# A weight block's wide and narrow products by turns, in a two-layer hybrid diffusion backbone

## The chip, the cores and the metric

The kernel runs on one core of one Trainium2 chip. The metric is the device time of one execution in microseconds. Before the change the median of three runs is 2560.39 us (2558.62 to 2562.19).

## The reference

Two layers over 512 latent tokens and 256 context tokens of width 1024, in float32. Each layer normalises the tokens with a modulation that comes from a conditioning vector, projects them once, and feeds three mixers side by side: windowed attention, a gated linear attention in chunks, and a two-dimensional neighbourhood attention. Their outputs are projected, gated by a sigmoid of the normalised input, summed and projected again; a SwiGLU feed-forward of hidden width 2816 follows. Cut to its frame:

```python
for layer in range(2):
    h = rmsnorm(x) * (1 + scale) + shift            # latents and context, own modulation
    p = h @ w_in[layer]                             # split among the three mixers
    y_a, y_b, y_c = window(p), linear(p), neighbourhood(p)
    gates = sigmoid(h @ w_merge + b_merge)          # three of width 1024
    x = x + gate * ((g_a * (y_a @ w_ba) + g_b * (y_b @ w_bb) + g_c * (y_c @ w_bc)) @ w_out)
    h = rmsnorm(x) * (1 + scale) + shift
    x = x + gate * ((silu(h @ w_gate) * (h @ w_up)) @ w_down)
```

In the second layer the context serves keys, values and the linear attention's state only; its later parts run over the 512 latents alone.

## The kernel before

Tokens lie along the free axis, features along the partitions. All big projections go through `gemm` (L370): one weight block holds 128 output features, with eight k tiles of 128 input features as a rule (four in the branch projections, `w_br`; six in the last part of the feed-forward's output). Float32 accuracy comes from splitting both operands into a high and a low half of type float32r: each k tile takes three products, `wh` with the high half of the tokens, `wh` with the low half, and `wl` with the high half. A moving operand is one of the token sets of the list `subs`: the 512 latents, called wide here, and where the context is needed the 256 context columns, called narrow. A set's products for one block form a chain that adds up in one PSUM bank; a copy out of the bank on ACT or DVE (`evac`) follows it.

A block runs the chain of the latents and then the chain of the context: 24 products and 24 products. PSUM buffers come from `gemm_psum` (L492). In the mixers there are three, named `g`; in the merge and the feed-forward (`wide`) four more, named `h`. The same `g` buffers hold the modulation vector of a later layer part while it adds up over eight small blocks (`ada`, `adp_tile`, L466 and L487), which `weave` spreads between the weight blocks of the mixers.

Weights come by DMA into `wr` (three buffers, queue SP), are cast to `wh` by ACT (L323), and `wl` is the rest, formed by DVE (L326). In the middle of each chain `ahead` starts the cast of a later block, and at the chain's end `split_lo` issues its low half and frees the raw block for the next DMA. At most two split blocks wait.

The emitter keeps a clock of TensorE's work. Generators (the linear attention, the norms, the stream of attention heads) are stepped by `tick` between products when their time has come, at the earliest each 0.5 us of that clock, and put their own products, copies and DVE work into the same engines' queues. All engines take their queues in order. A scheduler behind the emitter keeps its order as a rule; where products would wait for operands, as at the start of the merge, it lets the products of several blocks pass each other.

Copies out of the banks that the text speaks of: L554 and L559 (merge-gate logits, latents and context, one ACT copy each), L724 (projection blocks, one ACT copy), L1093 to L1110 (query and key stacks of the attention, four to ten ACT and DVE instructions).

Of the kernel before, what the change touches and what calls it, by code (L numbers as in the profile page):

```python
# [28 lines left out]
LEADQ = (1, 0)  # L29
LAG, GRAIN, QLAG = (0.7, 0.0, 0.5), 0.5, (0.0, 4.7)  # L30
# [5 lines left out]
# block numbers of the input projection after layout_inputs  # L36
AQ, AK, AV, GQ, GK, GV, GR, NQ, NK, NV = 0, 4, 5, 6, 8, 10, 14, 18, 22, 26
# sections of the modulation vector
# [3 lines left out]
def shape_constants():  # L42
    """Masks and rotary tables: functions of the shapes alone."""
    f = np.float32
# [40 lines left out]
def layout_inputs(i):  # L85
    """Reorders, slices and zero-pads the inputs; no value is changed."""
# [15 lines left out]
    # units of 1024 columns: two of halves of (shift, scale) of the mixer, then a section each  # L102
# [32 lines left out]
class Net:  # L135
# [23 lines left out]
    def psum_open(self, name, **bufs):  # L159
        """PSUM of a phase: s2 pairs of banks, p single ones."""  # L160
        self.pp = self.phx.enter_context(self.tc.tile_pool(name=name, bufs=bufs["s2"], space=PSUM))
# [4 lines left out]
    def hilo(self, hi, lo, src):  # L166
        """hi + lo == src, each with float32r's bits; src float32."""
        self.nc.scalar.copy(hi, src)  # L168
        self.nc.vector.tensor_tensor(out=lo, in0=src, in1=hi.bitcast(F32), op=ALU.subtract)

    def hilo_late(self, hi, lo, src):
        """hilo whose lo comes in the middle of the next product, when hi is there."""
        self.nc.scalar.copy(hi, src)  # L173
        self.late.append((lo, lambda: self.nc.vector.tensor_tensor(out=lo, in0=src, in1=hi.bitcast(F32),
                                                                   op=ALU.subtract)))
# [6 lines left out]
    def rsqrt(self, y, v, t):  # L182
        """y = v ** -0.5 (v > 0) by Newton steps from an exponent-halving start."""
# [13 lines left out]
    # The emitter keeps a clock of the tensor engine's work. Generators are fillers: each yields the time (us of  # L197
    # that clock) its next step's inputs need; the products between step them when it has passed.
# [18 lines left out]
    def tick(self):  # L217
        """Steps the fillers that are due; False if none was."""
# [24 lines left out]
    def room(self, what, limit):  # L243
        """Steps the fillers until fewer than limit of what are in use."""
        self.until(lambda: self.live.get(what, 0) < limit)

    def attend(self, units, delay=0.0):
        """Queues units of a head for the attention stream."""
# [8 lines left out]
    def stream(self):  # L257
        """Scores of a unit, values product of the head before, transposes of the unit before, by turns."""
# [31 lines left out]
    def run_items(self):  # L290
        """Runs the items in order; weight blocks are loaded and split ahead of the product that takes them."""
# [17 lines left out]
        def split_hi(k):  # L309
            """Splits the next block, if it is due by block k and has room; its lo part with split_lo."""  # L310
# [59 lines left out]
    def gemm(self, w, nk, subs):  # L370
        """subs: (moving(kt) -> (hi, lo), columns, evacuate(psum))."""
        def sub(wh, wl, mov, n, evac):
            ps = self.gemm_psum()
            for kt in range(nk):
                xh, xl = mov(kt)
                if any(lo.tensor is xl.tensor for lo, _ in self.late):
# [3 lines left out]
                self.matmul(ps[:, :n], wh[:, s], xh, start=kt == 0, stop=False)  # L380
                self.matmul(ps[:, :n], wh[:, s], xl, start=False, stop=False)
                self.matmul(ps[:, :n], wl[:, s], xh, start=False, stop=last)
# [3 lines left out]
                if self.clock > self.ticked + self.grain and not last:  # L386
                    self.tick()
            self.split_lo()
# [3 lines left out]
        def fn(wh, wl):  # L392
            for x in subs:
                sub(wh, wl, *x)
# [51 lines left out]
    def consts_rest(self):  # L446
# [12 lines left out]
        # relative biases shifted by the query's column i: [i, (layer, head, row offset), key column]  # L459
# [6 lines left out]
    def ada(self, l, units):  # L466
        """Units of the modulation vector of layer l: 1024 channels by eight items of a k tile; columns 256 g on
        go to rows 32 * g on."""
# [30 lines left out]
    def ada_cols(self, l, n, sb):  # L499
        nc = self.nc  # L500
        pm = self.O1()
        # [channel, (column group, half of it, stream)]
# [26 lines left out]
    def cap(self, f):  # L529
        """The items f adds, taken off the list."""  # L530
# [5 lines left out]
    def weave(self, main, side):  # L536
        """Adds main's items with side's spread between the GEMM blocks."""
# [11 lines left out]
    def zgates(self, l, blocks, ntok):  # L549
        """Logits of the merge gates, kept in DRAM until the merge."""  # L550
# [16 lines left out]
    # Two sets of tokens: (first column, end, stream)  # L567
    SETS = (((0, SEQ, 0), (SEQ, NT, 1)), ((0, 256, 0), (256, SEQ, 0)))

    def sq_add(self, x, kt, c):  # L570
        """Adds the squares of x's columns c (feature tile kt) to the running sums of their set."""
# [12 lines left out]
    def rstd_rows(self, c):  # L584
        """Generator: rstd of the tokens c, the same on all partitions; self.rows: SBUF tile, columns c."""
# [25 lines left out]
    def norm(self, l, which, c, new, early=False):  # L611
        """Generator: modulated RMS norm of the tokens c of self.x into self.h, (hi, lo) tiles (new: allocates
        them)."""
# [9 lines left out]
        if early:  # L623
            # (x is read again later: scaled in place, while the modulation is still to come)
# [7 lines left out]
        for kt in range(KT):  # L632
# [7 lines left out]
            if kt % 2 == 0:  # L640
                # t + bi, as hi + lo
# [25 lines left out]
    def hmov(self, l, which, c):  # L667
        """Moving operand: the tokens c of the norm's output, once it is there."""
# [12 lines left out]
    def win(self, l, b, lat, ctx):  # L681
        """One block of the input projection; lat / ctx evacuate their columns (None: not needed)."""
# [33 lines left out]
    def in_block(self, l, b, dst, scale=1.0, ctx=True):  # L716
        """(weights, sub, subs): a block of the input projection, scaled, into the tile dst()."""
# [11 lines left out]
    def gla_lead(self, l):  # L729
        """The first blocks of the input projection, a token set after the other: the second set's norm runs  # L730
        beside the first's products."""
# [19 lines left out]
    def gemm_low(self, l, c, tile_):  # L751
        """The 32 columns of the decays' inner rank; k tile kt adds to rows 32 * (kt % 4) on (the sum over the
        four groups of rows is the next product's)."""
# [39 lines left out]
    def gate_r(self, l):  # L793
        """The output gate of the linear attention, kept in DRAM until the merge."""
# [25 lines left out]
    def gla_unit(self, l, u, slot, want_o):  # L820
        """u = 0, 1: the latents of head pair u, four chunks of 128; u = 2: the context of both pairs, two
        chunks each.  Blocks b of 128 tokens: b = chunk, or b = 2 * pair + chunk."""
# [3 lines left out]
        # slices of the [128, 512] unit: (columns of the unit, tile index, columns of the tile)  # L826
# [8 lines left out]
        # log decays (times 16)  # L835
# [23 lines left out]
        def qbd(n, f):  # L859
            """Writes f(out, rows, columns, tile, columns of the tile) for both heads of the pair."""  # L860
# [10 lines left out]
        def products(kap, qt, other=False):  # L871
            """Keys of each half of a chunk with the queries of that half (or of the other one):
            [token of the chunk, (block, head), query of the half]."""
# [32 lines left out]
        def prep(n, s):  # L906
            """Factors of level n (pairs of blocks of s), then the sums over blocks of 2 s."""
# [41 lines left out]
        # whole chunks: factors towards the state  # L949
# [26 lines left out]
        # states  # L976
# [17 lines left out]
        for d in range(2):  # L994
# [8 lines left out]
            else:  # L1003
                # context: states before the second chunk go to st[:, d, b]
# [740 lines left out]
```

## Time and profile before

| | |
|---|---|
| median of three runs | 2560.39 us |
| span of the profiled execution | 2559.8 us |
| TensorE busy (PE) | 2483.4 us, 97%, 14908 products |
| weight loads (PEld) | 2089.3 us, 82% |
| VectorE busy (DVE) | 1396.2 us, 55% |
| ScalarE busy (ACT) | 1041.1 us, 41% |
| GpSimd busy (POOL) | 353.7 us, 14% |

The span runs from the first to the last instruction of one profiled execution; its own time is not given apart from the span, and the timed runs lie within 3 us of it. A matmul's printed duration includes the way through the array and overlaps the next one, so the distance from one start to the next is what it costs. In a time line, neighbouring rows of one kind are merged, also products of both widths if their names agree (the form shown is then the first one's), and the count stands behind the `x`. A product of plain float32, as those of the modulation vector, counts twice in it.

### The profile page before, as it was taken

The page shows a single profiled execution, that of the slowest core. Times are in us where ns is not written, and L with a number is a line of the kernel's source. Part 1 is how long each engine was busy: PE and PEld are TensorE (multiplying, and loading weights), DVE is VectorE, ACT ScalarE, POOL GpSimd, SP SyncE. Part 2 cuts the span into 40 slices and gives each one's busy share as a digit, 9 for nine tenths or more (in the row PEclk, how much of TensorE's full clock was granted, in tenths as well). Part 3 has the DMA queues.
Part 4 walks back from the last instruction along what each step waited for, and adds up shares of the span by engine and source line. Part 5 has one row for each costly group of instructions (what it writes and reads, how often), then busy time and mean ns, then how long its engine had stood idle before and what let it go on. Part 6 is the DMA issues. An engine that isn't in the chain of part 4 may idle for free.

```text
span 2559.8 us, 38398 instructions
## 1 busy us (share of the span) xinstructions
PE 2483.4 (97%) x14908; PEld 2089.3 (82%) x14908; DVE 1396.2 (55%) x2832; ACT 1041.1 (41%) x1717; POOL 353.7 (14%) x447
## 2 busy tenths in 40 slices
PE   6999999999999999999999999999999999999998
PEld 3777878888888888888888877677888879988887
DVE  4683547647656674222232377746657668633336
ACT  3533336545565353212212255434545565522223
POOL 0230204213212010000000022212313220000000
PEclk9999999999999999999999999999999999999999
DMA  6333452232337332221221243453332275432333
GB/s 219 123 119 121 159 165 86 85 120 81 88 131 244 126 116 91 66 65 59 66 66 58 86 135 127 152 186 113 103 95 80 81 239 182 156 99 96 94 95 120
DMA packets 116422, 300.44 MB, mean 117 GB/s; under 512 B 21520, under 2 KB 31504, under 8 KB 116240
## 3 DMA queue, kind: packets, MB, share of 16 engines
q1 hardware_dynamic: 116240, 297.99, 36.5%
q8 instruction: 117, 1.92, 0.3%
q14 instruction: 65, 0.53, 0.1%
HBM read 258.61 MB, written 29.57 MB: 113 GB/s over the span
## 4 chain that ended last, share of the span: by engine, by line
PE 82%; DVE 10%; ACT 4%; issue 1%; DMA 1%; SPq 0%; POOL 0%; DVEq 0%; ACTq 0%; POOLq 0%
PE g L211 44%; PE h L211 26%; PE s L211 5%; PE s L215 3%; PE o L211 3%; DVE qbd L918 2%; DVE wl L326 1%; PE p L211 1%; DVE T L582 1%; DVE T L645 0%; ACT wh L323 0%; DVE SS L928 0%; DVE PP L930 0%; DVE PP L929 0%; DVE T L626 0%
## 5 line engine op out<-in xcount | busy, mean ns | idle before, releaser
L211 PE MATMUL g<-T,wh 128*128 128x512 f32 (+1 forms) x4684 | 1237.3, 352 | 6.6 <-ACT wh L323 3.4
L211 PEld LDWEIGHTS g<-T,wh 128*128 128x128 f32 x4684 | 801.5, 190 | 129.4 <-issue 20.4
L211 PE MATMUL g<-T,wl 128*128 128x512 f32 (+1 forms) x2342 | 816.1, 349 | 11.4 <-DVE wl L326 11.3
L211 PE MATMUL h<-T,wh 128*128 128x512 f32 (+1 forms) x2612 | 660.2, 343 | 4.9 <-ACT T L168 4.7
L323 ACT CAST wh<-wr 128x1024 fp32r<-128x1024 f32 (+2 forms) x355 | 344.4, 971 | 686.8 <-PE h L211 268.0
L326 DVE TENSOR_TENSOR wl<-wr,wh 128x1024 fp32r<-128x1024 f32 (+2 forms) x355 | 403.6, 1137 | 360.4 <-ACT wh L323 346.9
L211 PEld LDWEIGHTS h<-T,wh 128*128 128x128 f32 x2612 | 450.5, 189 | 70.9 <-ACT T L168 6.5
L211 PEld LDWEIGHTS g<-T,wl 128*128 128x128 f32 x2342 | 444.6, 190 | 72.3 <-DVE wl L326 15.1
L211 PE MATMUL h<-T,wl 128*128 128x512 f32 (+1 forms) x1306 | 447.6, 343 | 2.5 <-DVE wl L326 2.5
L211 PEld LDWEIGHTS h<-T,wl 128*128 128x128 f32 x1306 | 247.2, 189 | 32.9 <-DVE wl L326 2.9
L1270 ACT ACTIVATE P<-P,sm 128x513 f32<-128x513 f32 (+3 forms) x160 | 115.9, 725 | 127.8 <-DVE sm L1312 113.6
L1275 POOL TENSOR_SCALAR P<-P,sm 128x512 f32<-128x512 f32 (+1 forms) x160 | 113.4, 710 | 386.3 <-DVE sm L1274 363.8
L652 POOL TENSOR_TENSOR T<-T,T 128x256 f32<-128x256 f32 (+1 forms) x24 | 30.0, 1272 | 731.6 <-DVE T L1555 532.0
L1325 DVE TENSOR_TENSOR ptl<-s,pth 128x512 fp32r<-128x512 f32 (+1 forms) x144 | 107.9, 749 | 39.2 <-ACT pth L1324 38.0
L1324 ACT CAST pth<-s 128x512 fp32r<-128x512 f32 (+1 forms) x144 | 90.6, 629 | 46.8 <-PE s L215 43.4
L1555 DVE SCALAR_TENSOR_TENSOR T<-h,mod,T 128x512 f32<-128x512 f32 (+1 forms) x64 | 38.4, 599 | 110.1 <-PE h L211 110.0
L215 PE MATMUL s<-k_ident,P 128*128 128x128 f32 x640 | 94.0, 274 | 1.7 <-POOL P L1275 1.2
L921 POOL TENSOR_TENSOR E<-E,T 128x512 f32<-128x512 f32 (+1 forms) x42 | 59.5, 1426 | 247.1 <-ACT E L917 209.7
L173 ACT CAST T<-T 128x512 fp32r<-128x512 f32 (+1 forms) x93 | 49.1, 535 | 107.0 <-DVE T L1574 100.0
L215 PEld LDWEIGHTS s<-k_ident,P 128*128 128x128 f32 x640 | 74.6, 140 | 16.4 <-issue 4.8
L918 DVE TENSOR_TENSOR qbd<-E,T 64x512 f32<-64x512 f32 (+1 forms) x84 | 72.1, 871 | 3.6 <-ACT E L917 2.2
L211 PE MATMUL o<-pth,V 128*128 128x512 f32 (+2 forms) x224 | 72.5, 333 | 0.2 <-ACT pth L1324 0.2
(201 smaller groups left out, 2302.0 us busy)
## 6 DMA issues: line engine op xcount, KB each, us to landing
wr<-in_w_fi_dram SPq DMA_DIRECT2D x98, 512.0 KB, 3.6
wr<-in_w_ada_dram SPq DMA_DIRECT2D x80, 512.0 KB, 4.1
wr<-in_w_in_dram SPq DMA_DIRECT2D x65, 512.0 KB, 3.9
wr<-in_w_merge_dram SPq DMA_DIRECT2D x48, 512.0 KB, 4.2
wr<-in_w_out_dram SPq DMA_DIRECT2D x32, 512.0 KB, 3.6
wr<-in_w_fo_dram SPq DMA_DIRECT2D x32, 512.0 KB, 3.5
wr<-in_w_br_dram SPq DMA_DIRECT2D x48, 256.0 KB, 2.9
wr<-in_w_fo_dram SPq DMA_DIRECT2D x32, 384.0 KB, 3.1
```

The source lines that it names most:

```text
L173: self.nc.scalar.copy(hi, src)
L211: return self.nc.tensor.matmul(out, lhsT, rhs, **kw)
L215: return self.nc.tensor.transpose(out, src, self.ident)
L323: self.nc.scalar.copy(hi[:, :n], r[:, :n])
L326: self.nc.vector.tensor_tensor(out=lo[:, :n], in0=r[:, :n], in1=hi[:, :n].bitcast(F32), op=ALU.subtract)
L918: qt = qbd(n + 1, lambda o, r, c0, c1, q: V.tensor_tensor(out=o, in0=blk(ee[r, 0, c0:c1]), in1=blk(q), op=ALU.mult))
L921: P.tensor_tensor(out=ee[:, 1, c0:c1], in0=ee[:, 1, c0:c1], in1=self.gk[p][:, t0:t0 + c1 - c0], op=ALU.mult)
L1270: nc.scalar.activation(out=P_[:, o0:e1], in_=P_[:, o0:e1], func=AF.Exp, bias=nm_, accum_out=rz)
L1275: nc.gpsimd.tensor_scalar(out=P_[:, o0:o1], in0=P_[:, o0:o1], scalar1=rz, scalar2=1.0, op0=ALU.mult, op1=ALU.mult)
L1324: nc.scalar.copy(hi, src)
L1325: return lambda: VE.tensor_tensor(out=lo, in0=src, in1=hi.bitcast(F32), op=ALU.subtract)
L1555: self.nc.vector.scalar_tensor_tensor(out=x[:, c0:c1], in0=ps[:, :c1 - c0], scalar=self.mod[l][:, sec * 8 + j, s:s + 1], in1=x[:, c0:c1], ...
```

## The change

`gemm` now makes each set's chain a generator that stops after every product. A small loop starts the first chain, lets it run `BEHIND = 6` products, starts the second, and then takes one product of each by turns until both are done. A block with one set runs as before. The chains' other duties (`ahead` in the middle, `split_lo` and the copy out at the end, `tick`) stay with their chain. The PSUM buffer is now taken after the first `mov(kt)`.

```diff
+BEHIND = 6
...
     def gemm(self, w, nk, subs):
-        def sub(wh, wl, mov, n, evac):
-            ps = self.gemm_psum()
+        def chain(wh, wl, mov, n, evac):
+            ps = None
             for kt in range(nk):
                 xh, xl = mov(kt)
+                if ps is None:
+                    ps = self.gemm_psum()
...
                 self.matmul(ps[:, :n], wh[:, s], xh, start=kt == 0, stop=False)
+                yield
                 self.matmul(ps[:, :n], wh[:, s], xl, start=False, stop=False)
+                yield
                 self.matmul(ps[:, :n], wl[:, s], xh, start=False, stop=last)
                 if kt == nk // 2 - 1:
                     self.flush()
                     self.ahead(False)
                 if self.clock > self.ticked + self.grain and not last:
                     self.tick()
+                if not last:
+                    yield
             self.split_lo()
             evac(ps)
             self.tick()

         def fn(wh, wl):
-            for x in subs:
-                sub(wh, wl, *x)
+            todo = [chain(wh, wl, *x) for x in subs]
+            n, live = 0, []
+            while todo or live:
+                if todo and n >= (len(subs) - len(todo)) * BEHIND:
+                    live.append(todo.pop(0))
+                live = [g for g in live if next(g, 0) is None]
+                n += 1
         self.items.append(Item(fn, w, nk))
```

The rest of the diff takes comments and docstrings away; line numbers move by a few.

First place: TensorE, a block of merge-gate logits in the first layer's linear attention, where its second set begins. `g` is the result bank, `T` a token tile (high or low half), `wh` and `wl` the halves of the weight block. Before:

```order
L211 MATMUL g294_2308<-T70_386,wh285_2229 128x512
L211 MATMUL g294_2308<-T69_385,wl286_2230 128x512
L211 MATMUL g294_2308<-T71_390,wh285_2229 128x512
L211 MATMUL g294_2308<-T72_391,wh285_2229 128x512
L211 MATMUL g294_2308<-T71_390,wl286_2230 128x512
L211 MATMUL g299_2341<-T44_279,wh285_2229 128x256
L211 MATMUL g299_2341<-T45_280,wh285_2229 128x256
L211 MATMUL g299_2341<-T44_279,wl286_2230 128x256
```

After:

```order
L212 MATMUL g292_2288<-T46_283,wl287_2236 128x512
L212 MATMUL g292_2288<-T48_288,wh286_2235 128x512
L212 MATMUL g295_2316<-T44_279,wh286_2235 128x256
L212 MATMUL g292_2288<-T49_289,wh286_2235 128x512
L212 MATMUL g295_2316<-T45_280,wh286_2235 128x256
L212 MATMUL g292_2288<-T48_288,wl287_2236 128x512
L212 MATMUL g295_2316<-T44_279,wl287_2236 128x256
L212 MATMUL g292_2288<-T50_293,wh286_2235 128x512
L212 MATMUL g295_2316<-T46_283,wh286_2235 128x256
L212 MATMUL g292_2288<-T51_294,wh286_2235 128x512
L212 MATMUL g295_2316<-T47_284,wh286_2235 128x256
```

Before, the context's first product stands behind the latents' last one; after, it stands behind the latents' seventh, and from there on the two banks alternate (128x512 and 128x256).

Second place: TensorE, the end of the same block and the start of the next, whose first bank is `g307`. `g267` is the bank of the modulation vector, `p` a product of the linear attention. Before:

```order
L211 MATMUL g299_2341<-T70_386,wh285_2229 128x256
L211 MATMUL g299_2341<-T69_385,wl286_2230 128x256
L211 MATMUL g299_2341<-T71_390,wh285_2229 128x256
L211 MATMUL g299_2341<-T72_391,wh285_2229 128x256
L211 MATMUL g299_2341<-T71_390,wl286_2230 128x256
L211 MATMUL g267_2072<-wr287_2245,cpad_72 32x256 x4
L211 MATMUL g267_2072<-wr292_2300,cpad_72 32x256 x4
L211 MATMUL g307_2406<-T44_279,wh295_2321 128x512
```

After:

```order
L212 MATMUL g292_2288<-T71_390,wl287_2236 128x512
L212 MATMUL p300_2359<-qbd0_1_708,E285_2218 64x128 x8
L212 MATMUL g295_2316<-T67_380,wl287_2236 128x256
L212 MATMUL g295_2316<-T69_385,wh286_2235 128x256
L212 MATMUL g295_2316<-T70_386,wh286_2235 128x256
L212 MATMUL g295_2316<-T69_385,wl287_2236 128x256
L212 MATMUL g295_2316<-T71_390,wh286_2235 128x256
L212 MATMUL g295_2316<-T72_391,wh286_2235 128x256
L212 MATMUL g295_2316<-T71_390,wl287_2236 128x256
L212 MATMUL g267_2072<-wr288_2263,cpad_72 32x256 x4
L212 MATMUL g267_2072<-wr290_2280,cpad_72 32x256 x4
L212 MATMUL g307_2406<-T44_279,wh296_2327 128x512
```

Before, all 24 products of the context lie between the latents' last product and the next block; after, the latents' last product stands seven context products ahead of the block's end.

Third place: ACT, the copies out of the same two banks (`T298` and `T299` are the logits), among the weight cast and the exponentials of the linear attention. Before:

```order
L323 CAST wh295_2321<-wr293_2306 128x1024
L554 COPY T298_2339<-g294_2308 128x512
L916 ACTIVATE E301_2357<-PP261_2030 128x32x16
L917 ACTIVATE E301_2357<-SS262_2031 128x32x16
L559 COPY T298_2339<-g299_2341 128x256
```

After:

```order
L324 CAST wh296_2327<-wr291_2286 128x1024
L568 COPY T299_2357<-g292_2288 128x512
L930 ACTIVATE E301_2368<-PP262_2045 128x32x16
L931 ACTIVATE E301_2368<-SS263_2046 128x32x16
L573 COPY T299_2357<-g295_2316 128x256
```

The order on ACT is the same: the cast of a later block stands ahead of the copy of the latents, two exponentials ahead of the copy of the context.

## Rows read from the trace of the kernel before

**Rows 1.** The page, busy time of each engine, and granted clock in 40 slices:

```profile
PE 2483.4 (97%) x14908; PEld 2089.3 (82%) x14908; DVE 1396.2 (55%) x2832; ACT 1041.1 (41%) x1717; POOL 353.7 (14%) x447
...
PEclk9999999999999999999999999999999999999999
```

**Rows 2.** The page, chain that ended last, shares of the span by engine:

```profile
PE 82%; DVE 10%; ACT 4%; issue 1%; DMA 1%; SPq 0%; POOL 0%; DVEq 0%; ACTq 0%; POOLq 0%
```

**Rows 3.** Windows of the first layer: length, busy time of PE, PEld, DVE, ACT, POOL:

```profile
91.00:375.00 284.00, 272.39 (x1969) 218.35 (x1969) 164.58 (x285) 106.30 (x159) 52.04 (x49) 0.99 0.40 131
375.00:768.00 393.00, 387.42 (x2501) 340.38 (x2499) 249.72 (x745) 214.19 (x438) 100.09 (x169) 1.00 0.32 101
768.00:1504.00 736.00, 729.30 (x4185) 637.83 (x4186) 313.93 (x466) 221.45 (x325) 37.77 (x28) 1.00 0.31 97
```

**Rows 4.** Waits of PE over the span: us in total, times, longest:

```profile
PE g L211 <- DVE wl L326: 11.3, 8, 3.7
...
PE g L211 <- ACT T L554: 0.5, 1, 0.5
```

**Rows 5.** Time line of PE, feed-forward; start, length, instruction, count:

```profile
1002.23 0.40 PE L211 MATMUL h<-T,wh 128*128 128x256 f32 x2
...
1005.10 0.63 PE L211 MATMUL g<-T,wh 128*128 128x512 f32 x2
...
1010.57 0.28 PE L211 MATMUL g<-T,wh 128*128 128x256 f32 x1
```

**Rows 6.** Time line of PE, second product of the feed-forward:

```profile
1094.10 0.40 PE L211 MATMUL g<-T,wh 128*128 128x256 f32 x2
...
1096.82 0.62 PE L211 MATMUL g<-T,wh 128*128 128x512 f32 x2
...
1102.42 0.28 PE L211 MATMUL g<-T,wh 128*128 128x256 f32 x1
```

**Rows 7.** Time line of PE, start of the first layer's merge:

```profile
778.69 0.76 PE L211 MATMUL h<-T,wh 128*128 128x512 f32 x3
779.29 0.39 PE L211 MATMUL h<-T,wl 128*128 128x512 f32 x1
...
782.01 0.63 PE L211 MATMUL g<-T,wh 128*128 128x256 f32 x3
782.47 0.76 PE L211 MATMUL h<-T,wh 128*128 128x512 f32 x3
783.07 0.39 PE L211 MATMUL h<-T,wl 128*128 128x512 f32 x1
783.30 0.28 PE L211 MATMUL g<-T,wh 128*128 128x256 f32 x1
...
784.00 0.28 PE L211 MATMUL g<-T,wh 128*128 128x256 f32 x1
```

**Rows 8.** Time line of PE and ACT, one block of merge-gate logits:

```profile
265.79 0.73 PE L211 MATMUL g<-T,wh 128*128 128x512 f32 x2
...
271.97 0.39 PE L211 MATMUL g<-T,wl 128*128 128x512 f32 x1
...
274.70 1.05 ACT L323 CAST wh<-wr 128x1024 fp32r<-128x1024 f32 x1 [7.55 <-DMA wr<-in_w_merge_dram]
...
275.65 0.58 ACT L554 COPY T<-g 128x512 f32<-128x512 f32 x1
...
276.37 1.07 PE L211 MATMUL g<-wr,cpad 128*32 128x256 f32 x16
...
277.37 0.73 PE L211 MATMUL g<-T,wh 128*128 128x512 f32 x2
```

**Rows 9.** Waits of ACT, first layer's linear attention (91 to 375 us):

```profile
ACT wh L323 <- DMA wr<-in_w_merge_dram: 45.6, 9, 8.0
```

**Rows 10.** Time line of PE and DVE, one query block of the softmax attention:

```profile
573.86 0.39 PE L211 MATMUL g<-T,wl 128*128 128x512 f32 x1
...
576.45 0.92 DVE L1098 SCALAR_TENSOR_TENSOR Q<-g,Q 64x128 fp32r<-64x128 f32 x4 [0.66 <-ACT Q L1093]
```

## The prediction

> **What bounds the kernel now.** I read the page's busy times and slices first, then the windows by stage, then what TensorE waits for, and last the time line of TensorE. TensorE is busy for 2483.4 of 2559.8 us, at full granted clock in every slice [rows 1], and the chain that ended last runs through it for 82% [rows 2]. By stage it stands idle for 284.00 - 272.39 = 11.6 us in the first layer's linear attention, 393.00 - 387.42 = 5.6 in its softmax attention, and 736.00 - 729.30 = 6.7 in its merge and feed-forward [rows 3]. So whatever the products themselves gain or lose per piece goes to the end of the kernel nearly one to one, and any new wait of TensorE is added to it. Of existing waits, the largest that touches weight blocks is for the low half of a split weight, 11.3 us in 8 places; waits for a copy out of a result bank (line 554) come to 0.5 us in all [rows 4]. That second number is the one to watch.
>
> The durations printed for a matmul overlap, so I take start to start. In the feed-forward 24 products of 256 columns start between 1002.23 and 1005.10, 119.6 ns each, and the following 24 of 512 columns end their turn at 1010.57, 227.9 ns each [rows 5]. In the output part, where the moving tiles come from the other pool, it is 2.72/24 = 113.3 ns and 5.60/24 = 233.3 ns [rows 6]. One wide and one narrow product cost 347.5 ns in the one place and 346.6 in the other: the two kinds trade some 6 ns, and the sum hardly moves.
>
> **The change part by part.** No product, copy or DMA is added or removed. Of 355 weight blocks 145 have both sets: 51 before the first layer's merge, 80 in its merge and feed-forward, 14 in the second layer. In the order of the programs a narrow product is followed directly by a wide one 123 times before and 2199 times after, so 2076 pairs (312 of them on the second pool's tiles) now hand over singly instead of in runs.
>
> *Term 1, the turns on TensorE.* The trace holds a stretch where products already alternate, because at the start of the merge several blocks wait for the same operands. There three wide and three narrow products start between 782.01 and 783.07: 1.06/3 = 353.3 ns a pair; two-and-two, in the same stretch, 783.30 to 784.00 is 0.70/2 = 350 ns [rows 7]. Against 347.5 that is +5.8 and +2.5 ns. The low end is each kind at its best chain, 227.9 + 113.3 = 341.2 ns, or -6.3; the high end is the worst turn seen: two wide and one narrow product start from 778.69 to 779.29 [rows 7], so (600 - 113)/2 = 243 for a wide one, with 119.6 for a narrow one 363 ns, or +15.6. Over 2076 pairs: -13, +5, +12, +32 us. I take +12, since the change alternates singly as that row does.
>
> [...]
>
> *Term 2, result banks.* Outside merge and feed-forward there are three buffers `g`, and the modulation vector holds one for eight items at a time. Before, the wide chain's copy out had the whole narrow chain (24 x 119.6 = 2.9 us) as cover before the next block needs the buffer. After, only the narrow chain's last seven products (0.84 us) are left, plus the modulation products between blocks (276.37 to 277.37, 1.0 us for sixteen [rows 8]; often there are fewer). A copy that runs at once fits: 0.58 us (line 554, rows 8). But ACT takes its queue in order. In rows 8 the wide chain's last product starts at 271.97, and the copy is at 275.65, because the weight cast queued ahead of it waited until 274.70 for a DMA: out at 276.23, 4.3 us later. ACT waits so nine times for 45.6 us [rows 9]. Such a copy was free; if the delay counted from the chain's end, it would miss a cover of 1.8 us by 2.5 us, nine times, 22 us. I do not expect that: the cast's time is set by the DMA, and the wide chain now ends later (265.79 + 6.4 us of its own, + 2.0 us for seventeen narrow products between = 274.2), while the next block still starts at about 277.4; the copy is out by 276.3. I take 2 us for these nine, bounds 0 and 22. Besides these, query and key blocks of the attention have copies of four to ten instructions: the last product starts at 573.86 and the last DVE piece ends at 576.45 + 0.92 = 577.37, 3.5 us [rows 10]. Against covers of 1 to 4 us (these seven products plus what fillers and modulation put between) I count thirteen places that miss by some 0.5 us: 6 us, bounds 0 and 13. Together +8, between 0 and +35. Queued behind a waiting wide product are all fillers of TensorE, so ACT and DVE get that time to catch up; for that reason I stay at the low side.
>
> The Trainium skill, "Perfetto Trace Analysis", section "Matmuls", asks that independent groups rotate through different PSUM banks so that the copy of one overlaps the next group's products. It speaks against the change: one block now keeps two buffers open to its end. Before, rows 4 agree with it (0.5 us of waits); how much is lost after, no row shows.
>
> *Weight splitting, at nothing.* The low half is now issued after the wide chain's last product, about 2 us later in a block of 8.3 us, and the next weight DMA with it. The block that takes it is one to two blocks away, so a block's products hide it. If that cover went, the 11.3 us of rows 4 could double.
>
> *Fillers, at nothing.* Attention steps are put between products after every third pair (0.96 us of the emitter's clock instead of 0.64); the count of places where products give way to fillers stays 428 against 427, and the same work is left at the end of each stage.
>
> Sum: 12 + 8 = +20 us on a span of 2559.8, that is 2580. The runs' median 2560.39 lies 0.6 us above the span, so I forecast 2580 for the time.
>
> **The rivals.** A: *TensorE goes by columns alone.* For it: the pair's sum is 347.5 and 346.6 in two layouts that differ in each kind [rows 5, 6], and two-and-two turns cost 350. Then term 1 is between 0 and +5, term 2 stays under 4: 2556 to 2566, about 2563. Against it: 353.3 in the single turns. B, the other side: *single turns lock into each kind's faster pace*, wide at 227.9 after a narrow one, narrow at 113.3 after a wide one, -13 us over all 2076 pairs; it decides where a pair is under 345 ns, and with little of term 2 gives 2548 to 2553. For it: both paces exist in the trace. Against it: no stretch has both at once. C: *the copies out decide*: delay counts from the chain's end, term 2 at its 35, term 1 at 12 or more: 2607 to 2620. For it: the ACT waits of rows 9; against it: those waits end with a DMA and not with the chain. D: *most blocks do not alternate*, since the scheduler undoes it: the order shows 2199 turns, so I give it none.
>
> **How the numbers follow.** Forecast 0.58, A 0.20, B 0.11, C 0.11. About 0.2%, 5 us, is what a measurement of this kernel can tell from no change. Faster by more (under 2555.3) is B: 0.11. Within: most of A, 0.17. Slower: the rest, 0.72. The range leaves out half of B and most of C: 2556 would cut all of B, so 2552 to 2607; the forecast's own range is 2567 to 2600.
>
> **What would show it.** Right for term 1: start-to-start of alternating products in the feed-forward, about 353 ns a pair, and that stage longer by 5 to 8 us with no new idle time. Right for term 2: a row where a `g` product waits for line 554, 724, 1098 or 1110 of before, well above 0.5 us, all ahead of the merge. Wrong: a pair at 341 to 345 (B), at 348 with unchanged idle time (A), or more than 25 us of new waits ahead of the merge (C).

## The result and the profile after the change

The changed kernel takes 2586.95 us (median of 4 runs, 2584.79 to 2589.26) against 2561.05 us for the kernel before (4 runs, 2558.62 to 2562.19) on the same chip. The ratio is 1.0101, 95% interval 1.0088 to 1.0114: 25.9 us slower, between 22.5 and 29.2. The forecast was 2580, from 2552 to 2607. The profiled execution spans 2583.8 us against 2559.8, so it shows 24.0 us of the loss.

The page of the changed kernel, busy time of the engines and the chain that ended last by engine:

```profile
PE 2500.8 (97%) x14908; PEld 2088.8 (81%) x14908; DVE 1395.9 (54%) x2832; ACT 1037.8 (40%) x1715; POOL 356.3 (14%) x447
...
PE 81%; DVE 10%; ACT 4%; DMA 2%; issue 2%; SPq 1%; POOL 0%; DVEq 0%; ACTq 0%; POOLq 0%
```

Against [rows 1, 2] the same work keeps TensorE busy 17.4 us longer (2500.8 - 2483.4), and the rest of the 24.0, 6.6 us, is new idle time. (Busy time includes products at half clock, and short waits that the overlap of printed durations hides.) The engine that decides is the same. Four marks say where the time goes. They are instructions that both programs have: the first scores of the softmax attention, the first product of the merge, a block in the second layer (its first product after sixteen of the modulation vector), and the end of the span. Time line of TensorE, kernel before:

```profile
378.60 1.32 PE L211 MATMUL s<-T,Q 128*128 128x256 f32 x8 [2.06 <-DVE Q L1090]
...
768.12 0.50 PE L211 MATMUL h<-T,wh 128*128 128x512 f32 x1 [1.18 <-ACT T L168]
...
1605.64 0.73 PE L211 MATMUL g<-T,wh 128*128 128x512 f32 x2
```

The same three in the changed kernel (a line number is 1 to 14 higher there; the bracket is the idle time before the instruction and what ended it):

```profile
382.36 0.75 PE L212 MATMUL s<-T,Q 128*128 128x256 f32 x4 [4.36 <-DVE Q L1104]
...
782.58 0.50 PE L212 MATMUL h<-T,wh 128*128 128x512 f32 x1 [0.95 <-ACT T L169]
...
1625.70 0.73 PE L212 MATMUL g<-T,wh 128*128 128x512 f32 x2
```

They come 3.8, 14.5 and 20.1 us later, and the end 24.0. So the work up to the first scores lost 3.8 us, the softmax attention 10.7, merge and feed-forward 5.6, the rest of the second layer 3.9. (The first of these is uncertain by some 3 us: the first experiment below, with before's order in all of the mixers, reached the first scores at 375.67.) The third stretch also holds the first blocks of the second layer's mixers.

Windows of the changed kernel at the stages' new places, columns as in [rows 3]:

```profile
91.00:379.00 288.00, 275.17 (x1976) 219.66 (x1974) 163.71 (x285) 106.57 (x158) 52.86 (x49) 0.98 0.40 130
379.00:782.00 403.00, 390.96 (x2484) 339.93 (x2484) 248.25 (x742) 211.52 (x434) 99.26 (x169) 1.00 0.30 97
782.00:1518.00 736.00, 730.93 (x4156) 635.06 (x4156) 310.23 (x460) 216.10 (x317) 35.72 (x27) 1.00 0.30 97
```

TensorE stands idle for 288.00 - 275.17 = 12.8 us in the linear attention (before 11.6), for 403.00 - 390.96 = 12.0 in the softmax attention (before 5.6), and for 736.00 - 730.93 = 5.1 in merge and feed-forward (before 6.7). New waits stand in the softmax attention; the merge and feed-forward have none and are longer all the same. That is the split that the two terms of the forecast name.

**The turns.** Time line of TensorE, alternating products of the feed-forward; a row holds a few products of either width, since rows group by operation:

```profile
1020.58 0.85 PE L212 MATMUL g<-T,wh 128*128 128x512 f32 x4
...
1026.93 0.40 PE L212 MATMUL g<-T,wh 128*128 128x256 f32 x2
...
1113.62 0.86 PE L212 MATMUL g<-T,wh 128*128 128x512 f32 x4
...
1119.97 0.40 PE L212 MATMUL g<-T,wh 128*128 128x256 f32 x2
```

From 1020.58 to 1026.93 there are six groups of three pairs, 6.35/18 = 352.8 ns a pair; on the second pool's tiles, 1113.62 to 1119.97, again 6.35/18 = 352.8. Before it was 347.5 and 346.6 [rows 5, 6], so a pair costs 5.3 to 6.2 ns more. The three pairs that the merge's start showed before, 353.3 [rows 7], were a good guide to these stretches. Single turns within them differ by some ns either way; 352.8 is their mean.

**The waits.** What TensorE waited for over the span, changed kernel (us in total, times, longest):

```profile
PE g L212 <- DVE wl L327: 6.1, 7, 1.8
...
PE p L212 <- DVE T L913: 5.3, 1, 5.3
...
PE g L212 <- ACT T L738: 4.1, 4, 2.4
...
PE g L212 <- ACT T L568: 2.5, 2, 2.0
...
PE g L212 <- DVE Q L1112: 2.2, 2, 1.2
...
PE g L212 <- DVE T L1112: 1.3, 1, 1.3
...
PE g L212 <- DVE Q L1124: 0.8, 2, 0.6
...
PE g L212 <- DVE T L1124: 0.4, 1, 0.4
```

Line 568 is 554 of before: 2.5 us where there was 0.5 [rows 4]. Line 738 is 724 of before, and there, too, a copy out of a result bank held products up before the change, which the 0.5 us that the prediction watches leaves out:

```profile
PE g L211 <- ACT T L724: 2.4, 1, 2.4
```

It has become 4.1. Lines 1112 and 1124, the pieces that copy queries and keys out, held TensorE up for 2.2 + 1.3 + 0.8 + 0.4 = 4.7 us in six places; before they don't appear. One such place, time line of DVE and TensorE in the softmax attention:

```profile
409.18 1.81 DVE L1104 TENSOR_TENSOR Q<-X,Q 64x512 fp32r<-64x512 f32 x2 [0.34 <-ACT Q L1103]
...
411.03 0.43 DVE L1112 SCALAR_TENSOR_TENSOR Q<-g,Q 64x256 fp32r<-64x256 f32 x1
...
411.51 0.51 PE L212 MATMUL g<-T,wh 128*128 128x256 f32 x2 [1.19 <-DVE Q L1112]
```

The next block's second set wants a result buffer. The copy that frees it is one 0.43 us piece, but DVE takes its queue in order, and two pieces for another operand, 1.81 us together, stand ahead of it. TensorE has nothing but the waiting product at the head of its queue for 1.19 us. The Trainium skill, "Perfetto Trace Analysis", section "Matmuls", asks that groups rotate through banks so that a copy runs beside the next group's products; in this place the copy no longer fits beside them, and the 1.19 us are what it costs.

The largest single wait of a weight block before, 11.3 us for low halves in 8 places [rows 4], has become 6.1 in 7. In its place stands one of 5.3 us for a tile of the linear attention (line 913). DVE is busy for 5.27 of the 5.30 us of the new wait (first row of the next windows) and for all of the 3.6 us of the longest old one: it looks like a backlog of DVE that shows at another instruction.

**The clock after a wait.** Windows of the changed kernel around the two longest waits; the third number from the right is the granted clock:

```profile
128.80:134.10 5.30, 0.00 (x0) 0.03 (x1) 5.27 (x11) 1.15 (x2) 1.68 (x2) 0.97 0.45 179
134.10:136.60 2.50, 2.50 (x18) 2.08 (x18) 2.12 (x4) 0.44 (x1) 0.00 (x0) 0.50 0.00 0
...
382.30:385.00 2.70, 2.45 (x12) 2.23 (x13) 2.25 (x7) 1.17 (x3) 0.00 (x0) 0.62 0.11 29
385.00:390.00 5.00, 5.00 (x34) 4.87 (x34) 3.29 (x13) 2.59 (x6) 2.47 (x4) 0.87 0.16 39
```

and of the kernel before, behind the same first scores:

```profile
378.60:381.00 2.40, 2.40 (x19) 2.40 (x20) 2.34 (x7) 0.86 (x2) 0.00 (x0) 1.00 0.45 162
```

After 2.1 us of idleness TensorE went on at the full 2.4 GHz; after 4.3 and 5.3 us it went on at 1.2 GHz (0.50), or partly so, for a while. Behind the first scores that costs 2.70 x 0.38 + 5.00 x 0.13 = 1.7 us on top of the wait. The Trainium skill tells of this in "TensorE: Matmul & The Clock Gate", section "HAM oscillation — how this bites in real kernels": there a wait for a DMA makes the next products start at half clock. The rows behind the two longest waits agree.

But the length of a wait doesn't decide it alone. Three windows behind shorter waits, each of another kernel: 1.81 us ahead of the first scores with turns in the linear attention alone, 1.96 us for line 568 in the changed kernel, and 0.55 and 1.18 us ahead of the merge in the kernel before:

```profile
381.10:384.50 3.40, 3.40 (x17) 3.40 (x17) 1.77 (x11) 1.63 (x4) 0.00 (x0) 0.51 0.32 78
...
253.20:256.60 3.40, 3.37 (x9) 2.70 (x10) 3.00 (x5) 0.84 (x3) 1.36 (x1) 0.50 0.69 217
...
769.40:772.80 3.40, 3.40 (x12) 2.82 (x11) 2.47 (x4) 1.58 (x2) 0.00 (x0) 0.50 0.61 192
```

All three are at half clock, while behind the 2.4 us wait for line 724 before the granted clock is 1.00 (125.90 to 129.30). So the 1.7 us behind the first scores are what this execution shows; that the longer wait brought them isn't shown, since 1.81 us at the same place was followed by the same. The kernel before has such stretches too: the digit 9 of its page [rows 1] stands for 0.9 or more.

With (1 - granted clock) x length summed over rows of 5 us, the clock withheld 6.9 us in the first layer's mixers after the change, 3.5 before, and 5.1 in the run with turns in merge and feed-forward alone, whose mixers keep before's order. From the merge to the third mark it is the other way: 5.1 before, 1.7 after. So the 5.6 us lost there stand against a stretch that had 3.4 us more withheld, and nothing shows that the turns are the reason.

### The profile page after: what moved, and what is told of

It reads as the page before. It is cut to its first block, busy times and chain, and to the rows that moved or that the text cites. A ratio compares the mean times of both kernels' runs of the same rounds, so it can differ in the third digit from the quotient of the medians.

```text
span 2583.8 us, 38434 instructions
## 1 busy us (share of the span) xinstructions
PE 2500.8 (97%) x14908; PEld 2088.8 (81%) x14908; DVE 1395.9 (54%) x2832; ACT 1037.8 (40%) x1715; POOL 356.3 (14%) x447
## 4 chain that ended last, share of the span: by engine, by line
PE 81%; DVE 10%; ACT 4%; DMA 2%; issue 2%; SPq 1%; POOL 0%; DVEq 0%; ACTq 0%; POOLq 0%
PE g L212 43%; PE h L212 26%; PE s L212 4%; PE o L212 3%; PE s L216 3%; DVE qbd L932 2%; DVE wl L327 1%; PE p L212 1%; ACT wh L324 1%; DVE T L659 0%; DMA wr<-in_w_merge_dram 0%; DVE P L1305 0%; DVE SS L942 0%; DVE T L596 0%; DVE ptl L1339 0%
## 5 line engine op out<-in xcount | busy, mean ns | idle before, releaser
L212 PE MATMUL g<-T,wh 128*128 128x512 f32 (+1 forms) x4684 | 1197.6, 352 | 13.8 <-ACT T L738 4.1
L212 PEld LDWEIGHTS g<-T,wh 128*128 128x128 f32 x4684 | 775.6, 189 | 145.6 <-issue 17.8
L212 PE MATMUL g<-T,wl 128*128 128x512 f32 (+1 forms) x2342 | 763.5, 351 | 6.1 <-DVE wl L327 6.1
L327 DVE TENSOR_TENSOR wl<-wr,wh 128x1024 fp32r<-128x1024 f32 (+2 forms) x355 | 409.0, 1152 | 361.7 <-ACT wh L324 354.3
L212 PEld LDWEIGHTS h<-T,wh 128*128 128x128 f32 x2612 | 441.1, 188 | 73.2 <-ACT T L169 6.0
L212 PEld LDWEIGHTS g<-T,wl 128*128 128x128 f32 x2342 | 416.7, 189 | 71.0 <-DVE wl L327 9.2
L212 PE MATMUL h<-T,wl 128*128 128x512 f32 (+1 forms) x1306 | 422.5, 344 | 2.5 <-DVE wl L327 2.5
L212 PEld LDWEIGHTS h<-T,wl 128*128 128x128 f32 x1306 | 234.5, 188 | 33.8 <-DVE wl L327 2.9
L1588 DVE TENSOR_TENSOR T<-T,h 128x512 f32<-128x512 f32 (+1 forms) x39 | 22.6, 578 | 101.3 <-PE h L212 101.3
```

Source lines behind the costliest of these rows:

```text
L212: return self.nc.tensor.matmul(out, lhsT, rhs, **kw)
L327: self.nc.vector.tensor_tensor(out=lo[:, :n], in0=r[:, :n], in1=hi[:, :n].bitcast(F32), op=ALU.subtract)
```

## The experiments

The theory: two costs, the turns on TensorE (5 to 6 ns a pair, everywhere) and result buffers that are held to a block's end (mixers alone, where there are three). The chief rivals: that one of them does it all, and that the places where attention steps are issued do. All times stand against the kernel before, run beside them. The mixers hold 1016 of the 2076 added turns (370 in the linear attention, 646 in the softmax attention, both layers), merge and feed-forward the other 1060. The edits are of one line, the number of products by which the second set stays behind; 3 * nk is the whole first set, so no turns.

**Where.** Turns in merge and feed-forward alone:

```
-                if todo and n >= (len(subs) - len(todo)) * BEHIND:
+                if todo and n >= (len(subs) - len(todo)) * (BEHIND if self.wide else 3 * nk):
```

> Products take turns only in the merge and the feed-forward of the first layer, where seven PSUM buffers are in use; the mixers run one chain after the other as before. Theory (turn pace and waits in the mixers are two separate costs): the stretch from the first product of the merge to the end of the first feed-forward is 5 to 7 us longer than before, the mixers are as before, so 2565 to 2569. Rival (everything is lost to waits for buffers in the mixers, the pace of turns costs nothing): 2561, within 2 us of before. Second rival (most of it is the pace): 2575 or more.

Measured: 2568.66 us, ratio 1.0028 (1.0019 to 1.0036), 7.2 us. Its marks for merge and feed-forward:

```profile
766.51 0.50 PE L212 MATMUL h<-T,wh 128*128 128x512 f32 x1 [1.18 <-ACT T L169]
...
1612.13 0.73 PE L212 MATMUL g<-T,wh 128*128 128x512 f32 x2
```

That is 845.6 us, 8.1 more than before (837.5), with 5.1 us withheld by the clock in both; ahead of it nothing is longer (768.12 before). As the theory expected; both rivals' times lie outside the interval, 4.9 to 9.2 us.

Turns in the mixers alone (`3 * nk if self.wide else BEHIND`):

> Products take turns only in the mixers of both layers, six products behind; merge and feed-forward run one chain after the other. Theory (buffers): the mixers lose 15 to 20 us, of which turn pace is at most 5, so 2576 to 2582. Rival (turn pace alone, some 950 pairs at 5 ns): 2566.

Measured: 2580.6 us, ratio 1.0074 (1.0061 to 1.0087), 19.0 us. As the theory expected; the rival's 5 to 6 us lie outside the interval, 15.6 to 22.3. The two parts add up to 26.2 against 25.9 for the whole, so no effect of one on the other shows. The page of this run:

```profile
PE 2492.8 (97%) x14908; PEld 2088.9 (81%) x14908; DVE 1391.6 (54%) x2832; ACT 1039.3 (40%) x1715; POOL 356.7 (14%) x447
```

Its span is 2579.0 us, 19.2 more than before. TensorE is busy for 2492.8 - 2483.4 = 9.4 us of that, and idle for the other 9.8. From the first product of the merge (784.66) to the third mark (1621.07) it takes 836.4 us, with 1.7 us withheld, as in the changed kernel; that one takes 6.7 more. So the turns of merge and feed-forward cost 6.7 to 8.1 us at like clock.

The mixers were then divided by a flag that is set at the start of the softmax attention and cleared at the start of the linear attention (`BEHIND if self.att and not self.wide else 3 * nk`, and `3 * nk if self.att or self.wide else BEHIND`):

> The sets take turns only in the blocks of the softmax attention (646 of the 2076 added turns; both layers). In the profile after, PE stood idle there for 402.25 - 390.58 = 11.7 us (379 to 781.25 us) against 391.70 - 387.18 = 4.5 before, and its products took 3.4 us more. Theory (the late copies of query and key blocks, and the first attention tile that waits for them, carry most of the mixers' loss): 11 to 14 us over before, 2572 to 2575, with waits of 3 us or more for the copies of queries (line 1112) and 4 to 5 us ahead of the first scores. Rival (the loss goes by the number of turns in the mixers, 646 of 1016 of the 19 us seen with the mixers alone): 12 us, and then the next run gives 7.

> The sets take turns only in the blocks of the linear attention stage (370 of the added turns). In the profile after, PE stood idle there for 288.00 - 275.17 = 12.8 us (91 to 379 us) against 284.00 - 272.39 = 11.6 before. Theory (a wait for a linear-attention tile only takes the place of one for the low half of a weight, and the copies behind weight casts hide as forecast): 1 to 4 us over before, 2562 to 2565. Rival by the number of turns: 7 us, 2568. Rival by the nine copies behind casts: 8 us or more.

Measured: 2575.38 us, ratio 1.0055 (1.004 to 1.007), 14.1 us, and 2567.14 us, ratio 1.0021 (1.0012 to 1.0029), 5.4 us. The softmax attention carries the greater part, as the theory had it. The linear attention's 5.4 is above the theory's 4, a miss. The rival by the number of turns isn't ruled out by these two runs: its 12 and 7 us lie in both intervals (10.2 to 17.9 and 3.1 to 7.4). The eight us of the copies behind casts are ruled out. What TensorE waited for in the mixers with turns in the softmax attention alone (a line number is up to 2 higher in these two kernels):

```profile
PE s L212 <- DVE Q L1106: 4.7, 1, 4.7
...
PE g L212 <- DVE Q L1114: 2.2, 2, 1.2
...
PE g L212 <- DVE T L1114: 1.3, 1, 1.3
PE s L216 <- POOL P L1291: 1.3, 1, 1.3
PE s L216 <- DVE ptl L1341: 1.1, 3, 0.5
```

and with turns in the linear attention alone:

```profile
PE g L212 <- ACT T L739: 4.1, 4, 2.4
...
PE s L212 <- DVE Q L1106: 1.8, 1, 1.8
```

Each half has its own waits of the changed kernel, and the wait for the first scores grows only with the softmax attention's turns.

**How far behind.** In the mixers alone, one product behind, and fifteen (`3 * nk if self.wide else 1`, and 15):

> As the run with turns in the mixers only, but the second chain starts one product behind instead of six, so that after the wide chain's last product only one or two narrow products are left: cover 0.1 to 0.2 us instead of 0.84. Theory (buffers): each of about 60 block ends loses up to 0.6 us more of cover, 10 to 30 us more than with six behind: 2588 to 2608. Rival (the loss in the mixers comes from turn pace or from where the fillers fall, not from the cover): 23 pairs a block instead of 18, at most 2 us more: 2578 to 2584.

> As the run with turns in the mixers only, but fifteen products behind: cover 1.8 us after the wide chain's last product, and nine pairs a block. Theory (buffers): most waits for copies go, 2563 to 2569. Rival (turn pace): half of the loss with six behind stays, about 2570. Rival (position of fillers): no order between one, six and fifteen.

Measured: 2602.26 us, ratio 1.0154 (1.0136 to 1.0171), 39.4 us, and 2568.08 us, ratio 1.0026 (1.0015 to 1.0038), 6.7 us. Both came out as the theory expected. For fifteen the rival's half of the loss, 9.5 us, lies within the interval too (3.9 to 9.7); what speaks against it is the stage. From the first scores to the merge, by the marks above:

| second set behind by | 24 (before) | 15 | 6 | 1 |
|---|---|---|---|---|
| narrow products left as cover | 24, 2.9 us | 16, 1.9 us | 7, 0.8 us | 2, 0.2 us |
| softmax attention, us | 389.5 | 391.9 | 400.0 | 409.3 |

(The 6 is the kernel with turns in the mixers alone.) Each step costs more than its turns can: from 15 to 6 behind there are 9 more turns in each of at most 36 blocks, 1.7 us at 5.3 ns, and the stage grew by 8.1. In the four runs of the table the clock withheld 0, 0, 2.8 and 6.7 us of this stage (summed as above); without that the order stays. So the cover decides here, as the theory says. But the run with one behind must be read with care. A window of it:

```profile
350.00:375.00 25.00, 25.00 (x118) 20.73 (x117) 6.48 (x15) 4.60 (x7) 0.42 (x3) 0.75 0.24 74
```

TensorE was busy throughout, at a granted clock of 0.75; the last wait ahead of it was one of 1.6 us. Summed as above, the clock withheld 25.5 us in this kernel's first mixers, 22 more than before, and the profiled execution is 45.1 us longer than before (2604.9 against 2559.8). Its four timed runs show mean granted clocks of 0.984 to 0.989 where before's profiled run shows 0.992, so between 8 and 21 us of them go to the clock (an estimate: the difference times the span). The expected time came out, but in good part by something that the expectation didn't hold.

**Turns of three.** The full change, with a set giving way only after each k tile's three products (two `yield` lines taken out, and the second set `BEHIND // 3` such steps behind):

> The full change, but the chains give way after every k tile (three products) instead of after every product; the second is still six products behind. Theory: turn pace falls to that of runs or near it (348 to 350 ns a pair instead of 352), so the first merge and feed-forward lose 0 to 3 us instead of 5.6, and the buffers' waits in the mixers stay: 2579 to 2584. Rival (that two banks are open at once costs pace, however long the turns): 2587, as with single turns.

Measured: 2587.36 us, ratio 1.0097 (1.008 to 1.0113), 20.5 to 28.9 us over before: a miss by the median, and no gain that these four runs can tell. In its profile, time line of TensorE in the feed-forward:

```profile
1040.86 0.63 PE L212 MATMUL g<-T,wh 128*128 128x512 f32 x2
...
1046.11 0.40 PE L212 MATMUL h<-T,wh 128*128 128x256 f32 x2
```

Five groups of three wide and three narrow take 5.25 us, 350.0 ns a pair, as expected. Merge and feed-forward took 842.0 us there (791.66 to 1633.69), with the same 5.1 us withheld by the clock as before (837.5) and as with single turns there alone (845.6). So at like clock the longer turns gave back some 3.6 us in this stage. The whole doesn't show it: the profiled execution, the longest of the four, had a mean granted clock of 0.985 against 0.992 after the change, 18 us of 2594.7; the two executions at 0.990 and 0.992 took 2585.57 and 2584.86 us. Whether the lower clock is this kernel's own stays open.

**The places for attention steps.** The full change, but the first set's end is no longer such a place:

```
             evac(ps)
-            self.tick()
+            if len(live) == 1 and not todo:
+                self.tick()
```

> The full change, but the first set's end is no longer a place where products give way to attention steps; only the end of the block is. In the change these two places lie seven narrow products, 0.84 us, apart. Theory (result banks and turns decide, the places are worth nothing): 2583 to 2590 as after. Rival (attention steps issued twice within a microsecond wait for each other, and that is the rest of the loss): 2572 to 2580, with the waits of scores and transposes (lines 1289, 1339) gone.

Measured: 2585.22 us, ratio 1.0094 (1.0076 to 1.0112). As the theory expected; the second place is worth nothing that can be measured.

**Addresses.** The two paces of [rows 5, 6] belong to tiles of two pools, which lie differently against the weights. So the full change was run with the weights' buffers 64, 128 and 256 bytes further on (a scratch tile made 16, 32 and 64 columns wider; the traces hold no addresses):

> The full change with a 1 KB scratch tile made 64 bytes longer, so that all split weight blocks lie 64 bytes further against the token tiles; no instruction differs. Theory (the pace of a product depends on the addresses of its moving tile and of the weights that load beside it, taken by some remainder): paces in the feed-forward, 234.7 and 117.7 ns in turns and 227 and 120 or 233 and 113 in runs before, move by up to 7 ns, the time by up to 15 us either way. Rival (the two pools differ for another reason): all paces as before within 0.5 ns, and 2585 to 2589.

> As the run with 64 bytes, with 128. Theory: other paces again; if one remainder has both kinds at their faster pace, 227 and 113 ns, a pair is 340 and the time falls by 10 us or more against the change. Rival: no paces move.

> As the run with 64 bytes, with 256. Theory: other paces again. Rival: no paces move.

Measured, one run each: 2597.29, 2593.91 and 2586.99 us. What this shows stands in the last section; as a way to get the time back it failed. No version tried here beats the kernel before; the nearest are the two that keep most of the cover or all of it, at ratios of 1.0026 and 1.0028.

## Why the prediction was right

*Slower, and by about how much.* Forecast +20 us, measured 25.9 (22.5 to 29.2). Both causes were named with their stages, and each stands alone in an experiment.

*Term 1, the turns: right in kind and in the pair's price, too small as a sum.* The pair was to cost 353; it is 352.8 on either pool's tiles. Merge and feed-forward were to be 5 to 8 us longer without new idle time: 6.7 to 8.1 at like clock, 7.2 by times. (The profile's 5.6 is within the range too, but by luck, since the clock withheld less there.) Over all turns the forecast was 12; TensorE was busy 17.4 us longer. Some 2 us of that are half-clock time (over the whole span the clock withheld 21.8 us, 19.6 before). Whether the remaining surplus is turns that cost more than those of the two stretches, or waits that the overlap of durations hides, stays open.

*Rivals A and B: wrong.* In neither pool's stretch is the mean pair at 348 or under 345 ns. *Rival C: wrong in size.* New idle time is 6.6 us after the change and 9.8 with turns in the mixers alone, not 35: the delay doesn't count from the chain's end where a DMA sets the cast. The block of [rows 8] shows this. Time line of the changed kernel:

```profile
274.67 1.05 ACT L324 CAST wh<-wr 128x1024 fp32r<-128x1024 f32 x1 [5.06 <-DMA wr<-in_w_merge_dram]
274.99 0.39 PE L212 MATMUL g<-T,wl 128*128 128x512 f32 x1
...
275.63 0.58 ACT L568 COPY T<-g 128x512 f32<-128x512 f32 x1
...
278.35 0.73 PE L212 MATMUL g<-T,wh 128*128 128x512 f32 x2
```

The cast starts at 274.67 (before 274.70), the wide chain ends with the product of 274.99 (forecast 274.2), the copy is out at 276.21 (forecast 276.3), and the next block starts without a wait. The forecast for these nine blocks was 2 us. Line 568 shows 2.5 in all, but that they are so close is luck: neither of its two waits stands behind a cast that waited for a DMA. The longer one, 1.96 us, ends at 253.2, when the copy has stood behind a table load and two exponentials on ACT:

```profile
252.05 0.66 ACT L931 ACTIVATE E<-SS 128x512 f32<-128x512 f32 x1
252.60 0.57 ACT L568 COPY T<-g 128x512 f32<-128x512 f32 x1
```

The other, 0.5 us, ends at 174.46, behind an exponential. So the blocks whose casts wait for a DMA cost nothing that a wait shows, and a queue of ACT that the forecast didn't price cost the 2 us.

*Term 2, result buffers: right in kind; the mixers' sum too small.* For the mixers the forecast comes to 1016 turns at 5.8 ns, 5.9, and 8 for the copies, 13.9 us; measured 19.0 (15.6 to 22.3). The profile of that run, 9.4 us busy and 9.8 idle, puts 3.5 of the missing 5 us on the side of the turns (part of it half-clock time) and only 1.8 on the side of the waits. So the waits as a sum were nearly right, but not as forecast: the query and key pieces made 4.7 us in six places against 6 in thirteen, and the rest came from elsewhere. What went wrong is the end of that paragraph, where I stayed at the low side because ACT and DVE would catch up while TensorE waits. What waits behind isn't only work that can be late at no cost. The wide copy of a query also leads to the operand of the next scores, and these waited 4.4 us instead of 2.1; with turns in the linear attention alone they waited 1.8. That fits the forecast's own 2.0 us by which the wide chain ends later in its block. And transposes of the attention waited, 1.3 + 1.1 us in the rows with turns in the softmax attention alone; in that stage before, 0.2 us of such waits stand, and 0.7 of a values product that the change took away. Against these stand the waits for low halves, which fell.

*Weight splitting and the places for attention steps, at nothing: right.* Waits for low halves went from 11.3 to 6.1 us, not up; one place fewer per block changed nothing. But the 5.3 us for a tile of the linear attention is a wait of an attention step that the forecast doesn't have. How much of it takes the place of the 3.7 us wait for a low half isn't shown; that stage alone made 5.4 us (3.1 to 7.4) against a forecast of 2.1 + 2.

## What to carry to other kernels

When two accumulation chains take turns, look first at when each one's result is copied out and who wants that buffer, and the copied value, next: the first chain's copy loses the second chain as its cover. Price the cover against the in-order queue of the engine that copies, not against the copy's own time, and allow for a half-clock stretch behind a new wait of TensorE, which came behind some waits of 1.8 us here and not behind one of 2.4. For the turns themselves, a short stretch of the old trace in which products already alternate by chance gave the pair's price to within a nanosecond (353.3 against 352.8); compare the sum with TensorE's busy time on the page. And when you compare stages of two traces, compare their granted clock first.

## What the runs showed of the hardware

In these runs, how fast products follow each other depends on how wide the scratch tile ahead of the split weights is, and so, it seems, on where the weights lie against the moving tiles. Three of the second layer's runs of wide products; the changed kernel, weights where they were:

```profile
2279.77 0.62 PE L212 MATMUL g<-T,wh 128*128 128x512 f32 x2
...
2287.25 0.62 PE L212 MATMUL g<-T,wh 128*128 128x512 f32 x2
```

with the weights 64 bytes further on:

```profile
2279.70 0.63 PE L212 MATMUL g<-T,wh 128*128 128x512 f32 x2
...
2288.80 0.63 PE L212 MATMUL g<-T,wh 128*128 128x512 f32 x2
```

and 128 bytes further on:

```profile
2279.77 0.64 PE L212 MATMUL g<-T,wh 128*128 128x512 f32 x2
...
2288.84 0.62 PE L212 MATMUL g<-T,wh 128*128 128x512 f32 x2
```

33 products in 7.48 us are 226.7 ns each, 39 in 9.10 us 233.3, 39 in 9.07 us 232.6; at 256 bytes the kernel's time was after's again (2586.99). So two of three offsets cost the wide products 6 ns, 3%, and the trade of wide against narrow that [rows 5, 6] show between the pools (227.9 and 119.6, 233.3 and 113.3) looks like the same thing. What makes it so isn't shown: only four places were tried, one run each for the three new ones, all in the changed kernel. The Trainium skill, "TensorE: Matmul & The Clock Gate", section "Back-to-back issue gap", gives columns/2.4 + 2.5 ns for an isolated warm product, 215.8 ns at 512 columns, and about 131 ns for one in a stream of products with their weight loads. None of the three stretches above comes down to either.
